# Exchange of softmax statistics between two key layouts in a conformer and dilated-attention block

## The chip, the cores and the metric

The kernel runs on one core of a Trainium2 chip. Its time is the device time of one execution in microseconds (us); the runs of a kernel are given by their median.

## The reference

The program computes one block on 1024 tokens with 1024 features, in 32-bit floats: an RMS norm, one input projection, a convolution branch with a gate, an attention branch, a merge of the two through sigmoid gates, and a feed-forward part with a short convolution. The change lies in the attention branch. There, 16 heads of 64 features attend in three groups of (window, dilation), and the groups are mixed by a softmax of their log-sums:

```python
for window, dilation in DILATION_GROUPS:          # (128, 1), (512, 4), (2048, 16)
    o_g, lse_g = dilated_window_attention(q, k, v, slopes, window, dilation)
...
mix = jax.nn.softmax(jnp.stack(lses), axis=0)
o = jnp.einsum('gbsh,gbshd->bshd', mix, jnp.stack(outs))
```

This is one softmax over all keys that any group admits, with the number of groups that admit a key as its weight. The kernel computes it in this form: its mask holds the logarithm of that number and the distance penalty.

## The kernel before, in words

**Precision.** A 32-bit product is made of three products of rounded halves (high by high, high by low, low by high); `split` (line 83) makes a high part on ACT (L85) and the low part on DVE (L86).

**Attention** runs in a loop of slots (from line 1106): 16 heads, two halves of 512 queries, four slots each, so eight slots ("places" 0 to 7) a head, and a tail of 13 slots. In its slot a query tile of 128 is scored on PE (`score`, L924 and L925); DVE adds the mask and takes the least value (L928); ACT takes the exponential and its sum (`powers`, L966). Twelve slots later (`BACK`) the weights are transposed on PE (`flip`, L1014), split, and multiplied by the values one slot on (`weigh`, L1051 and L1052). Between these, projection products of another branch fill PE (`fill`).

The queries of the second half (512 to 1023) meet two kinds of keys, in two layouts. *Near* keys are scored with queries in natural order: tile i, partition p is query 128 i + p. *Far* keys, the first half, are met only at distances that are multiples of four; they are scored by residue, so that partition j, column r is query 4 j + r. POOL copies the residue form of query and keys (`by_residue`, L921). The far scores are place 4, the near ones places 5 to 7. So each query of the second half has two maxima and two sums, in two layouts, and each layout needs those of the other to scale its weights:

- `own[h]` holds the statistics of head h, `own[h][:, 0]` of near and `own[h][:, 1]` of far rows, four pairs to a partition; `other[h]` is to hold the same queries' statistics from the other layout. Both have two buffers.
- `give` (L985) writes one layout's statistics to a scratch tensor in DRAM, and `take` (L989) reads them back in the other layout: 4 KB each, 8 bytes an element on the side of the near layout, 32 on that of the far one. They are called in the slot that made them: far at place 4, near at place 7.
- `combine` (L994 to L999) forms the factors, on DVE with one exponential on ACT, at place 6 of the next head; `times` (L969) scales the weights on POOL, and the far weights are flipped two slots later.

**Output.** `result` copies a finished half of a head to SBUF and writes it out with two transfers of 64 partitions (L1064), one for each half of the values' precision, into two DRAM tensors. `o_fetch` reads two feature blocks of 128 from each of the two, 512 tokens wide (L90 for the one, L152 for the other), and `o_step` adds and splits them (L1089, L1085, L1082).

**What sets the order.** ACT, DVE and PE run in the order of the text (`manual_schedule`). SP, which issues nearly all transfers, and POOL are ordered by a planner that simulates the program and issues what its simulation holds ready; each engine then runs its list in order, so an instruction that waits holds up all behind it. The head loads (`head`, L152 and L749) are six of 256 KB and the mask, with two buffers each; the program asks for those of head h + 1 at place 1 of head h, and for the values (`values`) at place 5.

Of the kernel before, what the change touches and what calls it, by code (L numbers as in the profile page):

```python
# [13 lines left out]
F32 = mybir.dt.float32  # L14
F32R = mybir.dt.float32r
AF = mybir.ActivationFunctionType
ALU = mybir.AluOpType
# [4 lines left out]
P = 128  # L22
D = 1024
T = 1024
KT = D // P
H = 16
DH = 64
# [8 lines left out]
FRONT = (1, 1, 1, 1, 0, 1, 1, 1)  # L36
BEHIND = (1, 0, 0, 0, 1, 0, 1, 0)
BACK = 12
START = (1, 1, 1, 1, 0, 0, 0, 0, 0, 0, 0, 0)
TAIL = (1, 1)  # L40
PLAIN = (10, 11)
# [17 lines left out]
def block_kernel(ctx: ExitStack, tc: tile.TileContext, x, xT, x0, g2, pack, mask,  # L59
                 w_first, w_ch, w_qkv, w_co, w_ao, w_o, w_up, w_down, out):  # L60
    nc = tc.nc
    act, dve, pool, pe, sp = nc.scalar, nc.vector, nc.gpsimd, nc.tensor, nc.sync

    cst = ctx.enter_context(tc.tile_pool(name="cst", bufs=1))
    wp = ctx.enter_context(tc.tile_pool(name="wp", bufs=1))
    psA = ctx.enter_context(tc.tile_pool(name="psA", bufs=2, space=PSUM))
    psB = ctx.enter_context(tc.tile_pool(name="psB", bufs=4, space=PSUM))
    dr = ctx.enter_context(tc.tile_pool(name="dr", bufs=1, space=DRAM))
# [14 lines left out]
    def split(hi, lo, src):  # L83

        act.activation(hi, src, AF.Copy)  # L85
        dve.tensor_tensor(out=lo, in0=src, in1=hi.bitcast(F32), op=ALU.subtract)  # L86

    def stage(src, name):
        raw = wp.tile([P, 1024], F32, tag="raw", bufs=4, name=f"raw_{name}")
        sp.dma_start(raw.rearrange("p (a b) -> p a b", a=src.shape[1]) if len(src.shape) == 3 else raw, src)  # L90
        return raw
# [59 lines left out]
    def fetch(dst, src):  # L151
        sp.dma_start(dst.bitcast(F32), src.bitcast(F32))  # L152
# [2 lines left out]
    dq = [[dr.tile([P, 4, T], F32R, name=f"dq{i}_{a}") for a in range(2)] for i in range(2)]  # L155
    dk = [[dr.tile([P, 4, T], F32R, name=f"dk{i}_{a}") for a in range(2)] for i in range(2)]
    dv = [dr.tile([T, 8, P], F32R, name=f"dv{i}") for i in range(2)]
    dst_ = [[dr.tile([512, 2], F32, name=f"dst{i}_{h}") for h in range(H)] for i in range(2)]
    dh = dr.tile([P, KT, T], F32, name="dh")
    db12 = [dr.tile([P, 4, 512], F32R, name=f"db12_{i}") for i in range(2)]  # L160
    dgate = [dr.tile([P, T], F32, name=f"dgate{i}") for i in range(16)]
    da = dr.tile([P, KT, T], F32, name="da")
    dya = [dr.tile([P, T], F32, name=f"dya{i}") for i in range(8)]
    do_ = [dr.tile([P, KT, T], F32, name=f"do{i}") for i in range(2)]
    dff = [dr.tile([P, T], F32, name=f"dff{i}") for i in range(FT)]
    dx2 = [dr.tile([P, D], F32, name=f"dx2_{i}") for i in range(8)]
    dform = [[dr.tile([P, 1024], F32R, name=f"dform{f}_{i}") for i in range(7)] for f in range(3)]
# [136 lines left out]
    if True:  # L304
# [156 lines left out]
        a, b = range(4), range(4, 8)  # L461
# [174 lines left out]
        for ch in range(6):  # L636
            kind, g8 = ch % 3, ch // 3
            wpieces = [wpiece(w_qkv[kind * 2 + g8, :, 2 * j : 2 * j + 2, :], f"qkv{ch}_{j}") for j in range(4)]
            for tt in range(8):
# [3 lines left out]
                if len(tails) > LAG:  # L643
                    t = tails.pop(0)
# [251 lines left out]
    if True:  # L896
# [80 lines left out]
        own, other = {}, {}  # L977
# [2 lines left out]
            own[h] = ready2("own", [P, 2, 4, 2], F32, 2, f"own_{h}")  # L980
            other[h] = ready2("other", [P, 2, 4, 2], F32, 2, f"other_{h}")

        def give(h, layout):
            d = dst_[layout][h]
            sp.dma_start((near_of, far_of)[layout](d), own[h][:, layout])  # L985

        def take(h, layout):
            d = dst_[1 - layout][h]
            sp.dma_start(other[h][:, layout], (near_of, far_of)[layout](d))  # L989

        def combine(h):
            o, t = own.pop(h), other.pop(h)
# [14 lines left out]
        def flip(h, half, group):  # L1007
            pp = bank_ps(f"pp_{h}_{half}_{group[0]}")
            ph = ready2("ph", [P, 512], F32R, 3, f"ph_{h}_{half}_{group[0]}")
            pl = ready2("pl", [P, 512], F32R, 3, f"pl_{h}_{half}_{group[0]}")  # L1010
            uses = []

            def turn(n, pt):
                pe.transpose(pp[:, n * P : (n + 1) * P], pt, ident)  # L1014

            if group == ("far",):
                for r in range(4):
                    turn(r, pts[h, "far", r][0])
                    uses.append((("far", r), slice(r * P, (r + 1) * P)))
                c = slice(0, 512)  # L1020
            else:
                used = []
                for kt in group:
                    q0 = max(kt, 4 * half)
                    q1 = 5 if kt == 3 and half else 4 * half + 4
                    first = 0 if kt == 3 and half else 1 if kt % 4 == 3 else q0 - 4 * half
                    for n, i in enumerate(range(q0, q1)):
                        turn(first + n, pts[h, i][0][:, (kt - lowest(i)) * P : (kt - lowest(i) + 1) * P])
                    cols = slice(first * P, (first + q1 - q0) * P)
                    uses.append(((kt, slice((q0 - 4 * half) * P, (q1 - 4 * half) * P)), cols))  # L1030
                    used.append(cols)
                c = slice(min(u.start for u in used), max(u.stop for u in used))
            order, runs = ((lambda t: t, lambda t: t) if group == ("far",) else
                           (by_fourth, lambda t: t.rearrange("p (i r a) -> p i r a", r=4, a=32)))
            split(runs(ph[:, c]), runs(pl[:, c]), order(pp[:, c]))
            return h, half, group, ph, pl, uses

        outs, read_out = {}, {}
# [15 lines left out]
            return (h, half) if last else None  # L1054

        def result(h, half):
            r = (h % 2) * DH
            o = outs.pop((h, half))
            cs = slice(half * 512, half * 512 + 512)
            tmp = ready2("ot", [P, 512], F32, 2, f"ot_{h}_{half}")  # L1060
            read_out[h, half] = act.activation(tmp.rearrange("p (i a r) -> p i a r", i=4, r=4),
                                               o.rearrange("p (i r a) -> p i a r", i=4, r=4), AF.Copy)
            for i in range(2):
                sp.dma_start(do_[i][r : r + DH, h // 2, cs], tmp[i * DH : (i + 1) * DH, :])  # L1064

        def fill(n):
            for _ in range(n):
# [3 lines left out]

        def o_fetch(half, k):
            cs = slice(half * 512, half * 512 + 512)
            raw = stage(do_[0][:, k : k + 2, cs], f"o_{half}{k}").rearrange("p (a b) -> p a b", a=2)
            hi, lo = (oT[i][half][:, k : k + 2, :] for i in range(2))
            fetch(lo, do_[1][:, k : k + 2, cs])
            return raw, hi, lo

        def o_step(new):
# [21 lines left out]
        with tc.manual_schedule(engines={ENG.Activation, ENG.DVE, ENG.PE}):  # L1101
            pend = []
            fill(1)
            for at in range(len(slots) + BACK + 1):
                count[2] += 1
                cur = slots[at] if at < len(slots) else None
                front, behind = (FRONT[at % 8], BEHIND[at % 8] + (START[at] if at < BACK else 0)) if cur else TAIL
                new = []
                if cur is not None:
                    h, half, n = cur  # L1110
                    place = at % 8
                    if place == 4:
                        statistics(h)
                    if place == 5:
                        values(h)
                    if place == 1 and h + 1 < H:
                        tiles[h + 1] = head(h + 1)
                    new = score(h, tiles[h], SCORES[half][n])
                for unit in late:
                    share(*unit)  # L1120
                if len(pieces) > 2:
                    piece_high(2)
                fill(front)
                if cur is not None and place == 6 and h + 1 < H or at == 1:
                    by_residue(h + 1 if at > 1 else 0)
                flips = []
                if BACK <= at < len(slots) + BACK:
                    fh, fhalf, fn = slots[at - BACK]
                    if FLIPS[fhalf][fn]:
                        flips.append(flip(fh, fhalf, FLIPS[fhalf][fn]))  # L1130
                for w in pend:
                    done = weigh(*w) or done
                pend = flips
                late = []
                if done is not None:
                    result(*done)
                    done = None
                since = at - BACK + 2
                if 0 <= since < len(slots) and slots[since][1:] == (1, 0):
                    combine(slots[since][0])  # L1140
                for unit in new:
                    powers(*unit)
                if cur is not None and half == 0:
                    late = new
                elif cur is not None and n in (0, 3):
                    give(h, 1 if n == 0 else 0)
                    take(h, 0 if n == 0 else 1)
                if at == len(slots):
                    p2_cm.__exit__(None, None, None)
                    hb2.append(ctx.enter_context(tc.tile_pool(name="hb2a", bufs=1, reuse_waits="tile")))  # L1150
                    oT = [[hb2[0].tile([P, KT, 512], F32R, tag=f"hb{a}0", name=f"oT{a}0")] for a in range(2)]
                    heads = [o_fetch(0, k) for k in range(0, KT - 2, 2)]
                if at > len(slots):
                    o_step(heads)
                if at == len(slots) + BACK - 4:
                    heads.append(o_fetch(0, KT - 2))
                piece_low()
                fill(behind)
                piece_high(2)
            for _ in gates:  # L1160
                piece_low()
                piece_high()
                o_step(heads)
# [325 lines left out]
    if True:  # L1489
# [49 lines left out]
        for f in range(FT):  # L1539
# [12 lines left out]
            r = ready.pop(0)  # L1552
# [235 lines left out]
```

## Time and profile before

| | |
|---|---|
| runs, median (lowest to highest of 3) | 1788.17 us (1788.1 to 1790.8) |
| the profiled execution | 1791.29 us, span 1789.2 us, mean granted clock 0.983 |
| PE busy / DVE / ACT / POOL | 1744.3 / 1300.4 / 789.1 / 223.7 us |
| HBM read / written | 214.80 / 84.02 MB |

The span is the time from the first to the last instruction of the profiled execution. "Busy" counts an engine's instructions, without those that only wait or issue transfers. The granted clock is the share of TensorE's full rate that was let through. In a row of groups stand the source line, the engine, the operation and out<-in by the program's names; in a row of waits, who waited for whom, the total in us, the times and the longest. SPq is SP's queue of issues.

### The profile page before, as it was taken

The numbers are of one execution on the slowest core, as the hardware profiler recorded it, in microseconds if no ns is written. First come the engines' busy times: TensorE is split into PE (matmuls) and PEld (weight loads), VectorE is DVE, ScalarE is ACT, GpSimd is POOL, SyncE is SP. The second block draws the span as 40 slices with busy tenths as digits, with TensorE's granted clock in tenths as the row PEclk, the third lists the DMA queues.
The fourth block names the chain that finished last, engine by engine and source line by source line (L and its number), as shares of the span: only waits on it lengthen the run. The fifth ranks groups of instructions, "written<-read, shape, count | busy, mean of one in ns | idle before, by whom it ended". The sixth has DMA issues, their size and how long they took to land.

```text
span 1789.2 us, 22776 instructions
## 1 busy us (share of the span) xinstructions
PE 1744.3 (97%) x8003; PEld 1422.1 (79%) x8003; DVE 1300.4 (73%) x2098; ACT 789.1 (44%) x1351; POOL 223.7 (13%) x300
## 2 busy tenths in 40 slices
PE   9999999999999997889899999999999999999999
PEld 7888888888888786777677888888888888888887
DVE  5999999999866465655455764687777677689863
ACT  5421233223335565656554643454454454543431
POOL 0000231132000344334330000000000000000000
PEclk9999999999999998889899999999999999999999
DMA  9311145345537878877766867542222222389851
GB/s 375 133 45 48 52 130 167 104 139 168 194 117 240 272 181 203 216 180 176 187 161 227 291 225 277 185 149 83 83 83 83 83 81 85 119 319 343 285 181 47
DMA packets 189938, 300.33 MB, mean 168 GB/s; under 512 B 35072, under 2 KB 93056, under 8 KB 189312
## 3 DMA queue, kind: packets, MB, share of 16 engines
q1 hardware_dynamic: 187376, 292.46, 51.0%
q10 hardware_dynamic: 2448, 6.42, 0.9%
q8 instruction: 63, 1.03, 0.2%
q14 instruction: 51, 0.42, 0.1%
HBM read 214.80 MB, written 84.02 MB: 167 GB/s over the span
## 4 chain that ended last, share of the span: by engine, by line
PE 88%; DMA 8%; DVE 1%; POOL 1%; ACT 1%; issue 1%; SPq 0%; ACTq 0%; DVEq 0%; POOLq 0%
PE dx L1594 7%; PE xz L141 6%; PE xz L142 6%; PE xz L143 6%; PE dy L1594 5%; PE qkv L134 5%; PE qkv L136 5%; PE qkv L135 5%; DMA dst<-own 4%; PE y L142 2%; PE y L141 2%; PE y L143 2%; PE wo L135 2%; PE wo L134 2%; PE wo L136 2%; PE yb L117 2%
## 5 line engine op out<-in xcount | busy, mean ns | idle before, releaser
L134 PE MATMUL qkv<-hi_qkv,hT 128*128 128x512 f32 x384 | 153.1, 400 | 0.0
L135 PE MATMUL qkv<-lo_qkv,hT 128*128 128x512 f32 x384 | 151.8, 396 | 0.0
L136 PE MATMUL qkv<-hi_qkv,hT 128*128 128x512 f32 x384 | 151.7, 396 | 0.0
L1497 DVE SCALAR_TENSOR_TENSOR u<-u,pk 128x1023 f32<-128x1023 f32 x88 | 112.2, 1277 | 1.2 <-ACT u L1495 1.1
L86 DVE TENSOR_TENSOR pl<-pp,ph 128x512 fp32r<-128x512 f32 (+1 forms) x95 | 59.2, 623 | 70.3 <-ACT ph L85 69.8
L110 POOL TENSOR_TENSOR rs<-ss,mhalf 128x8 f32<-128x8 f32 x32 | 66.3, 2073 | 303.4 <-DVE ss L109 303.3
L584 DVE SCALAR_TENSOR_TENSOR cacc<-csum,both,cacc 128x512 f32<-128x512 f32 x120 | 89.4, 745 | 0.3
L584 DVE SCALAR_TENSOR_TENSOR cacc<-apad,pk,cacc 128x512 f32<-128x512 f32 x120 | 88.3, 745 | 0.0
L136 PEld LDWEIGHTS qkv<-hi_qkv,hT 128*128 128x128 f32 x384 | 72.0, 188 | 17.1
L135 PEld LDWEIGHTS qkv<-lo_qkv,hT 128*128 128x128 f32 x384 | 72.1, 188 | 16.4
L134 PEld LDWEIGHTS qkv<-hi_qkv,hT 128*128 128x128 f32 x384 | 72.0, 188 | 16.4
L86 DVE TENSOR_TENSOR lo_uv<-raw_uv,hi_uv 128x1024 fp32r<-128x1024 f32 x20 | 24.5, 1225 | 82.1 <-ACT hi_uv L85 82.1
L584 DVE SCALAR_TENSOR_TENSOR codd<-apad,pk,codd 128x513 f32<-128x513 f32 x112 | 83.7, 748 | 0.7 <-ACT codd L577 0.7
L85 ACT ACTIVATE ph<-pp 128x512 fp32r<-128x512 f32 (+1 forms) x95 | 51.5, 542 | 58.4 <-PE pp L1014 55.9
L142 PE MATMUL xz<-blk_t,hi_s3g 128*128 128x512 f32 x176 | 69.3, 394 | 0.0
L141 PE MATMUL xz<-blk_t,hi_s3g 128*128 128x512 f32 x176 | 69.3, 394 | 0.0
L143 PE MATMUL xz<-blk_t,lo_s3g 128*128 128x512 f32 x176 | 69.0, 392 | 0.0
L141 PE MATMUL xz<-h2left,hi_uv 128*128 128x512 f32 x176 | 68.9, 391 | 0.0
L143 PE MATMUL xz<-h2left,lo_uv 128*128 128x512 f32 x176 | 68.6, 390 | 0.0
L142 PE MATMUL xz<-h2left,hi_uv 128*128 128x512 f32 x176 | 68.5, 389 | 0.0
L1495 ACT ACTIVATE u<-u,pk 128x1024 f32<-128x1024 f32 x44 | 54.6, 1240 | 9.2 <-DVE u L1484 4.5
L117 PE MATMUL ya<-aT,hi_co 128*128 128x512 f32 x128 | 57.5, 449 | 0.0
(486 smaller groups left out, 5155.6 us busy)
## 6 DMA issues: line engine op xcount, KB each, us to landing
wr<-w_down SPq DMA_DIRECT2D x45, 512.0 KB, 6.0
gr<-dff SPq DMA_DIRECT2D x62, 256.0 KB, 5.3
raw_qkv<-w_qkv SPq DMA_DIRECT2D x24, 512.0 KB, 5.2
dff<-u SPq DMA_DIRECT2D x22, 512.0 KB, 2.6
raw_uv<-w_up SPq DMA_DIRECT2D x21, 512.0 KB, 3.2
raw_ug<-w_up SPq DMA_DIRECT2D x20, 512.0 KB, 3.2
dv<-v SPq DMA_DIRECT2D x16, 512.0 KB, 2.8
q<-dq SPq DMA_DIRECT2D x32, 256.0 KB, 5.5
```

The source lines that it names most:

```text
L86: dve.tensor_tensor(out=lo, in0=src, in1=hi.bitcast(F32), op=ALU.subtract)
L110: pool.tensor_tensor(out=dst, in0=tmp, in1=mhalf[:, : tmp.shape[1]], op=ALU.pow)
L117: pe.matmul(o, hi[:, k, :], ah[:, k, :], start=(k == 0), stop=False)
L134: pe.matmul(ps, ah, hi[:, k % 2, :], start=(k == 0), stop=False)
L135: pe.matmul(ps, ah, lo[:, k % 2, :], start=False, stop=False)
L136: pe.matmul(ps, al, hi[:, k % 2, :], start=False, stop=(k == KT - 1))
L141: pe.matmul(o, wh[:, k, :], bh[:, k, :], start=(start and k == 0), stop=False, skip_group_check=not start)
L142: pe.matmul(o, wh[:, k, :], bl[:, k, :], start=False, stop=False, skip_group_check=not start)
L143: end = pe.matmul(o, wl[:, k, :], bh[:, k, :], start=False, stop=(k == 3), skip_group_check=not start)
L584: dve.scalar_tensor_tensor(out=out_, in0=src[:, i : i + size], scalar=w(i), in1=out_, op0=ALU.mult, op1=ALU.add)
L1497: dve.scalar_tensor_tensor(out=acc[:, d:], in0=src[:, : T - d], scalar=w(2 - d), in1=acc[:, d:], op0=ALU.mult, op1=ALU.add)
L1594: pe.matmul(banks[n][:, cols], a[:, c], b[:, d], start=(start and i == 0 and m == 0), stop=(stop and i == nf - 1 and m == 2), skip_group_c ...
```

## The change

- The near statistics are no longer written to DRAM. `near_to_far` copies them from `own` to `other` within SBUF, in four transfers, one for each query tile, each to 32 partitions.
- The far statistics still go through DRAM (`far_out`, `far_to_near`). The write is placed one slot after the far scores (`ago` 1), the readback five slots after them (1 + `TAKE`). `near_to_far` stands one slot after the last near scores.
- The output tensor in DRAM is one, ordered by head and precision half; `result` writes 128 partitions in one transfer, and `o_fetch` reads with four transfers of 64 partitions instead of two of 128.
- The call of `split` in `flip` is written out.

```diff
+TAKE = 4
...
-    dst_ = [[dr.tile([512, 2], F32, name=f"dst{i}_{h}") for h in range(H)] for i in range(2)]
+    dst_ = [dr.tile([512, 2], F32, name=f"dst_{h}") for h in range(H)]
...
-    do_ = [dr.tile([P, KT, T], F32, name=f"do{i}") for i in range(2)]
+    do_ = dr.tile([H, 2, DH, T], F32, name="do")
...
-        def give(h, layout):
-            d = dst_[layout][h]
-            sp.dma_start((near_of, far_of)[layout](d), own[h][:, layout])
-
-        def take(h, layout):
-            d = dst_[1 - layout][h]
-            sp.dma_start(other[h][:, layout], (near_of, far_of)[layout](d))
+        def near_to_far(h):
+            for i in range(4):
+                sp.dma_start(other[h][32 * i : 32 * i + 32, 1], own[h][:, 0, i])
+
+        def far_out(h):
+            sp.dma_start(far_of(dst_[h]), own[h][:, 1])
+
+        def far_to_near(h):
+            sp.dma_start(other[h][:, 0], near_of(dst_[h]))
...
-            split(runs(ph[:, c]), runs(pl[:, c]), order(pp[:, c]))
+            act.activation(runs(ph[:, c]), order(pp[:, c]), AF.Copy)
+            dve.tensor_tensor(out=runs(pl[:, c]), in0=order(pp[:, c]), in1=runs(ph[:, c]).bitcast(F32), op=ALU.subtract)
...
-            for i in range(2):
-                sp.dma_start(do_[i][r : r + DH, h // 2, cs], tmp[i * DH : (i + 1) * DH, :])
+            sp.dma_start(do_[h].rearrange("i d t -> (i d) t")[:, cs], tmp)
...
-            raw = stage(do_[0][:, k : k + 2, cs], f"o_{half}{k}").rearrange("p (a b) -> p a b", a=2)
+            raw = wp.tile([P, 1024], F32, tag="raw", bufs=4, name=f"raw_o_{half}{k}").rearrange("p (a b) -> p a b", a=2)
...
-            fetch(lo, do_[1][:, k : k + 2, cs])
+            for i, t in ((0, raw), (1, lo)):
+                for e in range(2):
+                    fetch(t[e * DH : (e + 1) * DH],
+                          do_.rearrange("(a e) i d t -> e i d a t", e=2)[e, i, :, k : k + 2, cs])
...
-                elif cur is not None and n in (0, 3):
-                    give(h, 1 if n == 0 else 0)
-                    take(h, 0 if n == 0 else 1)
+                for ago, n0, send in ((1, 0, far_out), (1, 3, near_to_far), (1 + TAKE, 0, far_to_near)):
+                    if 0 <= at - ago < len(slots) and slots[at - ago][1:] == (1, n0):
+                        send(slots[at - ago][0])
```

More of the change, by code (lines that the diff above doesn't have):

```diff
@@ L1056, in result @@
         def result(h, half):
-            r = (h % 2) * DH
             o = outs.pop((h, half))
```

## The prediction

> **What bounds the kernel now.** I read the page first, for the stretch in which the kernel loses time, then the busy time by head, then the waits, then SP's timeline.
>
> ```profile
> span 1789.2 us, 22776 instructions
> PE 1744.3 (97%) x8003; PEld 1422.1 (79%) x8003; DVE 1300.4 (73%) x2098; ACT 789.1 (44%) x1351; POOL 223.7 (13%) x300
> PEclk9999999999999998889899999999999999999999
> PE 88%; DMA 8%; DVE 1%; POOL 1%; ACT 1%; issue 1%; SPq 0%; ACTq 0%; DVEq 0%; POOLq 0%
> ```
>
> PE is the bound nearly everywhere. The only slices (some 45 us each) with a granted clock below nine tenths are the 16th to 18th and the 20th: attention, which runs from about 600 to 960 us. There the chain of waits names DMAs. The table by stage, cut where the far scores of each head begin, shows what a head costs; here are seven stretches of one head, one of the worst, and all fourteen from 612.1 to 917.4 us.
>
> ```profile
> core 0: us, PE busy (x) PEld busy (x) DVE busy (x) ACT busy (x) POOL busy (x), PEclk, DMA share, GB/s
> 634.80:652.40 17.60, 17.56 (x108) 14.77 (x107) 11.60 (x42) 13.14 (x39) 8.57 (x15) 1.00 0.71 176
> 652.40:671.40 19.00, 17.83 (x107) 14.81 (x107) 12.03 (x42) 12.74 (x38) 9.82 (x16) 1.00 0.64 172
> 744.20:765.00 20.80, 19.55 (x107) 16.14 (x107) 12.71 (x44) 12.86 (x39) 9.85 (x16) 0.92 0.75 208
> 765.00:786.20 21.20, 19.12 (x107) 15.99 (x106) 11.93 (x42) 12.48 (x38) 9.18 (x15) 0.92 0.69 171
> 833.40:851.90 18.50, 18.01 (x107) 14.88 (x107) 12.18 (x42) 13.01 (x39) 9.87 (x16) 1.00 0.71 175
> 851.90:877.90 26.00, 21.11 (x106) 17.13 (x105) 12.78 (x42) 12.98 (x39) 9.16 (x16) 0.87 0.80 192
> 877.90:899.00 21.10, 19.66 (x108) 16.09 (x107) 11.16 (x42) 12.20 (x37) 8.96 (x15) 0.92 0.81 184
> 899.00:917.40 18.40, 18.16 (x107) 14.83 (x106) 9.95 (x40) 12.01 (x36) 8.89 (x15) 1.00 0.60 150
> 612.10:917.40 305.30, 270.65 (x1466) 222.24 (x1465) 169.55 (x591) 179.93 (x524) 127.80 (x211) 0.91 0.76 188
> ```
>
> Every head has the same 106 to 108 matmuls, yet it takes 17.6 to 26.0 us. Four heads ran at clock 1.00 and take 18.4 us on average, 17.9 of them PE busy: PE's floor for a head. The mean is 305.3 / 14 = 21.8. What lies above the floor is PE idle (305.30 - 270.65 = 34.7 us) and half clock (0.09 of 305.3 is some 27 us; the two overlap a little). The floor for all fourteen would be 14 x 17.9 = 251: there are 54 us to win here, and no more.
>
> The waits in attention (595 to 985 us) say what PE and SP wait for:
>
> ```profile
> SPq L989 <- DMA dst<-own: 137.6, 32, 6.3
> DVE both L994 <- DMA other<-dst: 27.7, 10, 4.7
> PE pp_far L1014 <- POOL pf L969: 17.0, 11, 2.9
> PE s L925 <- DMA kl<-dk: 8.3, 6, 3.6
> PE o L1052 <- DVE pl L86: 5.2, 4, 2.5
> PE s L924 <- DMA kh<-dk: 3.5, 2, 2.2
> ```
>
> PE waits for weights that POOL scales late (pp_far), because DVE's combination (L994) waits for statistics, and for late K loads. Both come through SP, and SP stands 137.6 us before the 32 readbacks of L989, until the write issued just ahead has landed. One head of SP's timeline:
>
> ```profile
> 662.04 0.68 SPq L985 DMA_DIRECT2D dst<-own  x1
> 668.08 0.38 SPq L989 DMA_DIRECT2D other<-dst  x1
> ...
> 673.23 0.58 SPq L985 DMA_DIRECT2D dst<-own  x1
> 673.85 0.56 SPq L152 DMA_DIRECT2D kh<-dk  x1
> 674.46 0.59 SPq L152 DMA_DIRECT2D kl<-dk  x1
> 678.76 0.34 SPq L989 DMA_DIRECT2D other<-dst  x1
> ```
>
> SP stands from 662.7 to 668.1 (far pair) and from 675.1 to 678.8 (near pair), 9.1 of the 23 us to the next far write. The near stop lies in the middle of the next head's K loads, and it makes the near statistics two legs long. So in attention **SP's order is the bound**, and PE's gaps follow from it.
>
> **What the clock does with the gaps.** Three stretches around one late pp_far:
>
> ```profile
> 682.50:684.60 2.10, 0.02 (x2) 0.02 (x1) 1.73 (x8) 1.72 (x5) 1.10 (x3) 1.00 0.98 253
> 684.60:685.60 1.00, 0.64 (x2) 0.26 (x2) 1.00 (x6) 1.00 (x5) 1.00 (x2) 1.00 1.04 280
> 685.60:689.00 3.40, 3.21 (x9) 2.65 (x10) 1.60 (x4) 1.94 (x6) 2.63 (x6) 0.51 0.73 230
> ```
>
> A gap of about 2.1 us is followed by 3.4 us at 0.51 of the clock, so a removed gap brings back more than its length. [...]
>
> **The change, part by part.** Rows for it (tiles, then landings; durations are min/median/max in ns, the last column of a landing row is the median in us):
>
> ```profile
> L985 SPq DMA_DIRECT2D dst<-own x32: 340/547/1957, 604.1 to 928.5; - x32
> L989 SPq DMA_DIRECT2D other<-dst x32: 325/352/377, 610.5 to 932.8; - x32
> L1064 SPq DMA_DIRECT2D do<-ot x62: 445/588/2696, 638.2 to 967.1; - x62
> L152 SPq DMA_DIRECT2D oT<-do x8: 360/504/808, 929.2 to 972.8; - x8
> L90 SPq DMA_DIRECT2D raw_o<-do x8: 366/505/686, 839.1 to 971.6; - x8
> L928 DVE DVE_READ_ACCUMULATOR2_ANT own<- x128: 81/83/85, 602.2 to 927.0; 128x1 f32 x128
> do<-ot SPq DMA_DIRECT2D x62, 128.0 KB, 6.2
> q<-dq SPq DMA_DIRECT2D x28, 256.0 KB, 5.5
> dst<-own SPq DMA_DIRECT2D x32, 4.0 KB, 5.9
> other<-dst SPq DMA_DIRECT2D x32, 4.0 KB, 2.0
> ```
>
> 1. Near statistics. One write, one stop and one readback become four transfers with nothing to read back. The stop goes: 137.6 / 32 = 4.3 us a head. SP issues four instead of two. No row has a transfer inside the chip; its issue lies between the fastest readback, 0.33, and the slowest write, 1.96 us; I take the write's median, 0.55 (same source tile). So 4 x 0.55 - 0.55 - 0.35 = +1.3 us a head (ends +0.4 and +6.9). It lands after 1.5 to 8.9 us, the ends of the two kinds of rows; I take 5.9, as for the 4 KB write, which lands no sooner than the 256 KB loads beside it. Its new wait is for ACT's exponentials of the slot before; behind it on SP are the next head's K and Q halves and the mask. The combination is six slots later, 6 x 18.4 / 8 = 13.8 us, so even 8.9 fits.
>
> 2. Far statistics. Write and readback stay, so the two issues are the same, and the question is where SP takes the readback. SP's order is the planner's, not the program's: the first raw_o fetch issues at 839.1 us, while the program places it behind the last scores (927.0). So four slots later in the text is no promise; I count the far stop as kept, 4.3 us a head. Kept, it is cheap: it falls before the next K loads have their buffers. Behind it stand the V loads, which have twelve slots, and the output.
>
> 3. Output. One issue instead of two, twice a head: 2 x 0.59 = -1.2 us a head. The bytes are the same.
>
> 4. Fetches of the output, four instead of two, eight times: 16 more issues of 0.50. The low parts in the tail of attention hold up DVE (the wait of L1052 for pl, 5.2 us in 4), so one issue more delays them: two such places, +1 us. The eight of the second half stand ahead of loads for a later product: +4 us on SP, hidden behind the first projection products, which fill PE; uncovered it would cost those 4 us.
>
> 5. The call of split in flip is written out as the same two instructions: nothing on ACT, DVE or PE. POOL's order may change; within a head it is 9 us busy of 18, and I take nothing.
>
> **Sum.** SP gets 4.3 + 1.2 - 1.3 = 4.2 us a head back, plus what the near statistics' second leg (the 2.0 us landing, and 0.35) no longer adds to combinations that wait: I take 4.6. No head falls below 18.4. The three at 20.8, 21.2 and 21.1 gain 2.4 + 2.8 + 2.7 = 7.9; the four at 73.5 together nothing; the seven others, 305.3 - 73.5 - 63.1 = 168.7 us or 24.1 each, go to 19.5, which is 32.2. That is 40 us, less 1 for the tail: **39**. Against the profiled execution (1791.3, of which span 1789.2) that is 1752; the median of the runs shown is 3.1 lower, so the forecast is 1788.2 - 39 = **1749 us**. What is late next is PE itself, in heavy heads still SP with its far stop.
>
> **Rivals.**
> - *All stops go* (far too, if the planner does put other transfers between): all heads reach the 17.9 floor, 54 us: 1734, and 1730 with a little from the head after 917. For: four heads already run within 0.6 of it. Against: the planner's free order, and the loads still land 5 us after buffers come free.
> - *The gaps shrink, the clock or POOL stays.* Either pp_far stays late, because POOL's residue copies wait for K loads ahead of it (17.0 of the 39 us that PE waits), or half clock has another cause and only idle comes back (34.7 of 62). Both leave about 0.56 of 40: 22 us, 1766. [...] Against: the gap and half-clock rows.
> - *Nothing gained*: the planner moves the K loads behind the four transfers and SP is as late as before: 1788.
> - *Slower: the four transfers back up SP.* Place: ahead of the second K halves. If each issue takes as long as the slowest write, 1.96 us, they hold SP 7.8 us where the near pair held it 0.55 + 4.3 + 0.35 = 5.2; less 1.2 for the output, that is 1.4 a head, in fourteen heads 20 us, and half as much again by clock: 1818. It decides from (5.2 + 1.2) / 4 = 1.6 us an issue. Against: the median is 0.55.
>
> **How the numbers follow.** Forecast (1738 to 1757) 0.52; all stops go 0.11; partial (1757 to 1780) 0.22; nothing 0.05; slower 0.10. A measurement of this kernel tells about 0.2% (3.6 us) from no change. Faster 0.85, same 0.05, slower 0.10. The range takes the forecast, the partial case to 1777 and half of the case above it, from 1728.
>
> **What would show it.** Right: SP's wait for dst<-own falls from 137.6 to about 69 us or less; the copies from own to other issue in some 0.55 us; combinations no longer wait 27.7 us; PEclk in slices 16 to 20 rises to nine; heads take 18 to 20 us. Wrong: issues of over 1.6 us; a new wait of SP for ACT's exponentials of several us a head; K loads behind the four transfers with PE still waiting for kl; or the half clock without gaps.

## The result and the profile after

The changed kernel takes 1761.26 us (median of 4, 1759.65 to 1762.69) against 1788.13 us for the kernel before in the same session: 0.9846 of it, with a 95% interval of 0.9829 to 0.9863. It is faster by 27 us; 39 were forecast (1749, range 1728 to 1777). In a later session the kernel before took 1799.18 us and the changed one 1763.18: 0.9804 (0.9786 to 0.9822). The kernel before differs by 11 us between the two sessions, the changed one by 2. Why is not settled: in all four later sessions, on three chips, the kernel before took 1798.0 to 1799.2 us. So below, kernels of different sessions are compared by their ratios to the kernel before beside them.

The page of the changed kernel: PE and the granted clock.

```profile
span 1758.8 us, 22866 instructions
PE 1726.9 (98%) x8003; PEld 1409.3 (80%) x8003; DVE 1305.8 (74%) x2098; ACT 788.9 (45%) x1351; POOL 225.2 (13%) x300
PEclk9999999999999999999999999999999999999999
PE 88%; DMA 5%; DVE 2%; ACT 2%; SPq 1%; POOL 1%; issue 1%; ACTq 0%; DVEq 0%; POOLq 0%
```

No slice is below nine tenths any more. The table by stage, cut at the far scores of each head as before (the columns are those of the prediction's table), for two of the shortest heads, the three longest, and all fourteen:

```profile
629.20:646.20 17.00, 17.00 (x107) 14.72 (x106) 11.15 (x42) 13.15 (x39) 8.49 (x15) 1.00 0.80 201
721.40:742.60 21.20, 19.39 (x106) 16.12 (x106) 14.33 (x43) 12.83 (x39) 9.73 (x16) 0.92 0.83 221
742.60:763.40 20.80, 19.26 (x107) 16.09 (x106) 13.21 (x42) 12.41 (x38) 9.20 (x16) 0.92 0.82 214
819.60:845.80 26.20, 21.15 (x108) 17.31 (x107) 12.73 (x42) 13.11 (x39) 9.55 (x16) 0.87 0.86 209
864.00:881.00 17.00, 17.00 (x107) 14.84 (x106) 9.95 (x40) 12.08 (x36) 8.88 (x15) 1.00 0.57 146
611.80:881.00 269.20, 253.57 (x1466) 210.91 (x1465) 175.06 (x591) 180.11 (x524) 129.35 (x211) 0.97 0.83 212
```

The fourteen heads take 269.2 us where they took 305.3: 36.1 less. PE idle there fell from 34.7 to 15.6 us (269.20 - 253.57), and the mean clock rose from 0.91 to 0.97. But from the start of the sixteenth head to the end of the span the changed kernel takes 1758.8 - 881.0 = 877.8 us, and the kernel before 1789.2 - 917.4 = 871.8. So 36 us were won in the heads and **6 given back after them**, which makes the 30.4 us between the two spans (0.3 lies ahead of the heads). The waits of 595 to 985 us show both sides:

```profile
SPq L992 <- DMA dst<-own: 63.8, 15, 6.4
DVE both L997 <- DMA other<-dst: 0.9, 1, 0.9
PE pp_far L1017 <- POOL pf L970: 9.1, 10, 1.5
PE yb L118 <- DVE gg L1209: 7.3, 1, 7.3
PE s L926 <- DMA kl<-dk: 0.5, 1, 0.5
```

SP stands half as long before a readback (63.8 for 137.6 us). Combinations hardly wait (0.9 for 27.7), late K loads are gone (0.5 for 8.3), late far weights halved (9.1 for 17.0). New is one wait of 7.3 us for yb, a projection product after attention.

### The profile page after: what moved, and what is told of

The parts are those of the page before. It is cut to its first block, busy times and chain, and to the rows that moved or that the text cites. A ratio compares the mean times of both kernels' runs of the same rounds, so it can differ in the third digit from the quotient of the medians.

```text
span 1758.8 us, 22866 instructions
## 1 busy us (share of the span) xinstructions
PE 1726.9 (98%) x8003; PEld 1409.3 (80%) x8003; DVE 1305.8 (74%) x2098; ACT 788.9 (45%) x1351; POOL 225.2 (13%) x300
## 4 chain that ended last, share of the span: by engine, by line
PE 88%; DMA 5%; DVE 2%; ACT 2%; SPq 1%; POOL 1%; issue 1%; ACTq 0%; DVEq 0%; POOLq 0%
PE dx L1599 7%; PE xz L142 6%; PE xz L143 6%; PE xz L144 6%; PE dy L1599 5%; PE qkv L135 5%; PE qkv L136 5%; PE qkv L137 5%; PE y L143 2%; PE y L142 2%; PE y L144 2%; PE wo L136 2%; PE wo L135 2%; PE wo L137 2%; DMA oT<-do 1%; DMA kl<-dk 1%
## 5 line engine op out<-in xcount | busy, mean ns | idle before, releaser
L118 PE MATMUL yb<-oT,hi_ao 128*128 128x512 f32 x128 | 50.9, 398 | 7.3 <-DVE gg L1209 7.3
```

## The experiments

Each experiment is one kernel. "Heads" is the time from the first far score of the second head to that of the sixteenth, "rest" from there to the end of the span, both of the profiled execution, of which there is one for each kernel. Ratios are to the kernel before in the same session. Of the kernel before there is a trace from the first session only.

| kernel | median us | ratio (95%) | heads | rest |
|---|---|---|---|---|
| before (first session) | 1788.1 | | 305.3 | 871.8 |
| changed (first session) | 1761.3 | 0.9846 (0.9829 to 0.9863) | 269.2 | 877.8 |
| changed again | 1763.2 | 0.9804 (0.9786 to 0.9822) | 270.3 | 878.3 |
| near alone | 1760.2 | 0.9786 (0.9770 to 0.9801) | 276.9 | 870.7 |
| output alone | 1795.2 | 0.9979 (0.9968 to 0.9990) | 296.7 | 880.8 |
| TAKE 0 | 1767.1 | 0.9822 (0.9808 to 0.9837) | 277.5 | 878.7 |
| tensor by precision first | 1883.3 | 1.0471 (1.0455 to 1.0487) | 375.9 | 892.0 |
| stop kept | 1814.6 | 1.0090 (1.0071 to 1.0109) | 318.5 | 881.7 |
| far on chip too | 1750.6 | 0.9727 (0.9702 to 0.9752) | 261.8 | 877.8 |
| changed, old output | 1756.6 | 0.9767 (0.9748 to 0.9785) | 272.7 | 870.1 |
| fetches on two queues | 1767.2 | 0.9826 (0.9807 to 0.9846) | 275.2 | 878.4 |
| old output, far on chip | 1747.7 | 0.9726 (0.9704 to 0.9748) | 260.7 | 869.8 |
| the same, dya on SP | 1744.9 | 0.9704 (0.9685 to 0.9723) | 262.4 | 870.1 |
| old output, narrow fetches | 1770.4 | 0.9838 (0.9812 to 0.9864) | 277.5 | 880.7 |

**Which half pays: near alone, output alone.** To the kernel before was added only one part of the change: the near copies here, the one output tensor with its fetches there.

```diff
-                elif cur is not None and n in (0, 3):
-                    give(h, 1 if n == 0 else 0)
-                    take(h, 0 if n == 0 else 1)
+                elif cur is not None and n == 0:
+                    give(h, 1)
+                    take(h, 0)
+                elif cur is not None and n == 3:
+                    near_to_far(h)
```

> The kernel before with the near statistics alone sent on chip; far pair, output and fetches as before. Theory (SP's stop behind the near write is what pays, and the output half gives back in the tail what it wins in the heads): 1755 to 1767 us, SP's wait for dst<-own falls from 137.6 to some 65 us, PE's 7.3 us wait of yb does not appear. Rival (the single output transfer is what pays): above 1780 us.

> The kernel before with the output tensor, the single output transfer and the four fetches alone; both statistics pairs as before. Theory: 1780 to 1794 us, some 1 us a head won and 6 to 8 us lost behind the sixteen fetches of the second half, where PE waits for yb. Rival (the single output transfer is what pays): below 1772 us.

Near alone took 1760.2 us. Its ratio, 0.9786, cannot be told from that of the whole change in the later session (0.9804; the intervals overlap); SP's wait is 66.0 us, and there is no wait of yb. Output alone won 0.2%: its heads are short of 305.3 by 8.6 us, and its rest is 9.0 us longer, with PE's wait for yb at 6.6 us. Its median is 1 us above the expected range, in a session in which the kernel before was 11 us slower. So the near half is what pays. Whether it pays by the stop or by statistics that come sooner, these two kernels do not tell; the stop kept, below, does.

**The measure for the second group.** The changed kernel again.

> The changed kernel as it is, as the measure for the others of this group. Both theories: 0.980 to 0.987 of the kernel before.

It came out at 0.9804, within that.

**Stop or late statistics: the stop kept.** Behind the four transfers SP also writes the near statistics to a scratch tensor and reads them into a tile that nothing uses. What the output needs travels the short way, but SP stands.

```diff
+        def stop(h):
+            sp.dma_start(near_of(dummy[h]), own[h][:, 0])
+            sp.dma_start(p2b.tile([P, 4, 2], F32, tag="idle", bufs=2, name=f"idle_{h}"), far_of(dummy[h]))
...
-                for ago, n0, send in ((1, 0, far_out), (1, 3, near_to_far), (1 + TAKE, 0, far_to_near)):
+                for ago, n0, send in ((1, 0, far_out), (1, 3, near_to_far), (1, 3, stop), (1 + TAKE, 0, far_to_near)):
```

> The changed kernel, with a write of the near statistics to DRAM and a readback into a tile that nothing reads added behind the four transfers, so that SP stands again while the statistics still go the short way. Theory (the time comes from SP standing): 15 to 30 us above the changed kernel, SP's wait for dst and dummy some 60 us more. Rival (it comes from statistics that arrive sooner): within 5 us of the changed kernel.

It took 1814.6 us, 51 above the changed kernel beside it: the theory's direction, but far more than its 15 to 30. SP's waits, PE's for K loads, and the fourteen heads in this kernel:

```profile
SPq L997 <- DMA dst<-own: 73.1, 15, 6.0
SPq L991 <- DMA dummy<-own: 56.4, 16, 5.0
PE s L926 <- DMA kh<-dk: 13.8, 8, 2.6
PE s L927 <- DMA kl<-dk: 8.7, 10, 1.6
611.70:930.20 318.50, 278.52 (x1466) 228.16 (x1464) 164.42 (x591) 180.04 (x524) 126.00 (x211) 0.88 0.75 179
```

The heads grew by 48 us (318.5 for 270.3), while SP stands 60 us more (129.5 for 69.2). Late statistics are not the cause: DVE's combinations wait for them once, 4.6 us, and for a far pair. What is late is K: PE waits 22.5 us for it, where the changed kernel waited 0.5 for kl. SP stands nearly as long as in the kernel before (129.5 for 137.6), and issues eight transfers of statistics a head where that one issued four, so this kernel is slower still. That was the size the expectation missed: it priced the stop as the change had won it, and left out the issues. How much of the 51 us the two added issues take, and how much the standing, no kernel separates.

**Does the place in the text matter: TAKE 0.**

```diff
-TAKE = 4
+TAKE = 0
```

> The changed kernel with the far readback asked for in the slot of its write (TAKE 0 instead of 4). Theory (the planner sets SP's order, the text position does not): 1757 to 1766 us, as the changed kernel, with the same 60 to 68 us of SP wait for dst<-own. Rival (the four slots pay): above 1770 us and more wait of SP.

It took 1767.1 us, 1 us above the expected range; its ratio cannot be told from that of the changed kernel (the intervals overlap). SP's wait is nearly the same (72.5 us in 16, beside 69.2 in 15), if above the expected 60 to 68. What differs is the first head of the fourteen: 23.1 us at a granted clock of 0.85, where the changed kernel has 17.4 (at 1.00) and 18.5. There the planner's order did change: of SP's 911 issues one stands elsewhere in its list, the readback of the head before. So the four slots matter in one head out of fourteen; everywhere else the planner's order stood.

**Is the far stop free: far on chip too.** The far statistics go in four transfers, the other way round.

```diff
-        def far_out(h):
-            sp.dma_start(far_of(dst_[h]), own[h][:, 1])
...
-            sp.dma_start(other[h][:, 0], near_of(dst_[h]))
+            for i in range(4):
+                sp.dma_start(other[h][:, 0, i], own[h][32 * i : 32 * i + 32, 1])
...
-                for ago, n0, send in ((1, 0, far_out), (1, 3, near_to_far), (1 + TAKE, 0, far_to_near)):
+                for ago, n0, send in ((1, 0, far_to_near), (1, 3, near_to_far)):
```

> The changed kernel with the far statistics sent on chip as well, in four transfers, and no DRAM for either. Theory (each stop of SP costs): 4 to 12 us below the changed kernel, SP's wait for dst gone. Rival (the far stop stands where nothing is urgent): within 3 us of the changed kernel, or above it by the two further issues a head, 2 x 0.6 us.

It took 12.6 us less than the changed kernel (1750.6 for 1763.2), just beyond the expected 4 to 12; SP's wait for dst is gone, and the fourteen heads take 261.8 us. SP's timeline of the changed kernel shows what the far stop holds up:

```profile
651.02 0.63 SPq L989 DMA_DIRECT2D dst<-own  x1
651.86 0.61 SPq L986 DMA_DIRECT2D other<-own  x1
656.95 0.37 SPq L992 DMA_DIRECT2D other<-dst  x1
657.42 0.49 SPq L153 DMA_DIRECT2D kh<-dk  x1
```

and PE's in the same head, when K's buffer was last read:

```profile
653.63 0.28 PE L926 MATMUL s<-kl,q 128*128 128x256 f32 x1
```

The buffers were free at 653.9 us, and the K load went out at 657.4, behind the readback for which SP had stood since 652.5. So the far stop does lie across the K loads.

**Where the tail's 6 us go: four kernels.** The first was to undo the narrow fetches: a tensor ordered by precision half, then head, so that a fetch is two transfers of 128 partitions and the output stays one.

```diff
-    do_ = dr.tile([H, 2, DH, T], F32, name="do")
+    do_ = dr.tile([2, H, DH, T], F32, name="do")
...
-            sp.dma_start(do_[h].rearrange("i d t -> (i d) t")[:, cs], tmp)
+            sp.dma_start(do_[:, h, :, cs], tmp)
...
-                for e in range(2):
-                    fetch(t[e * DH : (e + 1) * DH],
-                          do_.rearrange("(a e) i d t -> e i d a t", e=2)[e, i, :, k : k + 2, cs])
+                fetch(t, do_[i].rearrange("(a e) d t -> (e d) a t", e=2)[:, k : k + 2, cs])
```

> The changed kernel with the output tensor ordered by precision half, then head, so that a fetch is two transfers of 128 partitions again and the output stays one transfer. Theory (the sixteen narrow fetches of the second half hold DVE and through it PE): 1750 to 1757 us, PE's wait for yb under 2 us. Rival (the wait comes from the bytes, or from SP being early): 1759 to 1764 us with the wait still there.

It took 4.7% more than the kernel before, and both theories were wrong about its time. What the DMA engines moved, in 40 slices of 630 to 900 us, and one stretch of those in which the rate is low:

```profile
GB/s 203 118 37 180 202 174 38 135 232 187 42 168 215 249 99 110 185 232 169 120 137 228 252 52 119 202 228 52 92 200 235 56 86 202 186 83 81 174 251 84
697.90:703.20 5.30, 5.30 (x30) 4.69 (x29) 2.44 (x8) 3.02 (x8) 2.54 (x5) 0.83 0.13 50
```

The rate breaks down to 37 to 56 GB/s again and again, with PE waiting for K loads (34.1 us in 5). The new write has 2 as its outermost size, where it was 128. In the stretch shown the share of busy DMA engines is 0.13 (the last number but one), by my estimate two of the sixteen engines at a time (0.13 x 16 = 2.1). But no row here names the engine of a packet, and whether the size of 2 sets this share is not shown. PE's wait for yb is gone in this kernel, as the theory said; with everything else late, that settles nothing, and the fetches' question stayed open.

The second put back the old output and fetches; the third issued half of the second half's fetches from ACT's queue.

```diff
-    do_ = dr.tile([H, 2, DH, T], F32, name="do")
+    do_ = [dr.tile([P, KT, T], F32, name=f"do{i}") for i in range(2)]
...
-            sp.dma_start(do_[h].rearrange("i d t -> (i d) t")[:, cs], tmp)
+            r = (h % 2) * DH
+            for i in range(2):
+                sp.dma_start(do_[i][r : r + DH, h // 2, cs], tmp[i * DH : (i + 1) * DH, :])
...
-                for e in range(2):
-                    fetch(t[e * DH : (e + 1) * DH],
-                          do_.rearrange("(a e) i d t -> e i d a t", e=2)[e, i, :, k : k + 2, cs])
+                fetch(t, do_[i][:, k : k + 2, cs])
```

```diff
-                    fetch(t[e * DH : (e + 1) * DH],
-                          do_.rearrange("(a e) i d t -> e i d a t", e=2)[e, i, :, k : k + 2, cs])
+                    (act if half and i else sp).dma_start(
+                        t[e * DH : (e + 1) * DH].bitcast(F32),
+                        do_.rearrange("(a e) i d t -> e i d a t", e=2)[e, i, :, k : k + 2, cs].bitcast(F32))
```

> The changed kernel with the output tensors, the two output transfers and the two fetches of before. Theory (the output half gives back in the tail what it wins in the heads): within 5 us of the changed kernel, with PE's 7 us wait of yb gone and the fourteen heads 5 to 9 us longer. Rival (the single output transfer is worth more than its tail): 6 us or more above it.

> The changed kernel with the eight fetches of low parts of the second half issued from ACT's queue instead of SP's. Theory (the tail is lost because SP issues sixteen narrow fetches one after the other): 3 to 8 us below the changed kernel's 1761 to 1763, and PE's wait for yb under 4 us. Rival (the bytes or their landing set the tail): within 2 us of it, the wait still 6 to 8 us.

The old output is 6.6 us **faster** than the changed kernel, 1.6 more than expected: its heads are 2.4 us longer (5 to 9 expected), its rest 8.2 us shorter, and the wait of yb is gone. The two queues changed nothing in the rest (878.4 us, wait of yb 7.7): the theory that SP's issuing sets the tail fell. (The median, 1767.2, lies 4 us above the changed kernel's, outside the rival's 2 us as well; the ratios cannot be told apart.) The DMA engines were full either way. The first 14.6 us of the second half's fetches, in the kernel before, the changed one, that with the old output and that with two queues:

```profile
967.80:982.40 14.60, 14.60 (x67) 12.07 (x66) 8.08 (x8) 4.07 (x5) 0.00 (x0) 1.00 1.01 362
```

```profile
926.90:941.50 14.60, 14.60 (x66) 12.09 (x65) 5.30 (x5) 2.72 (x3) 0.00 (x0) 1.00 1.00 254
```

```profile
933.00:947.60 14.60, 14.60 (x66) 12.07 (x65) 8.05 (x7) 3.70 (x5) 0.00 (x0) 1.00 1.01 357
```

```profile
934.20:948.80 14.60, 14.60 (x66) 12.11 (x65) 4.26 (x4) 2.62 (x3) 0.00 (x0) 1.00 1.02 245
```

The last two numbers are the DMA share and GB/s: busy all the time in each, but 245 to 254 GB/s with fetches of 64 partitions and 357 to 362 with 128. Width or the tensor's order in DRAM? The fourth kernel has the old tensors and output, and cuts only the fetches in two (shown against the kernel with the old output).

```diff
-            fetch(t, do_[i][:, k : k + 2, cs])
+            for e in range(2):
+                r = slice(e * DH, (e + 1) * DH)
+                fetch(t[r], do_[i][r, k : k + 2, cs])
```

> The changed kernel with the output tensors and the two output transfers of before, but each fetch still cut into 64 partitions (four transfers a step, as in the changed kernel). Theory (the width of the fetches sets their rate in the tail, where the DMA engines are busy all the time): PE's wait for yb is 6 to 8 us again, the stretch of the second half's fetches moves some 250 GB/s, 0.979 to 0.984 of the kernel before. Rival (the order of the output tensor in DRAM sets it): no wait of yb, some 360 GB/s, 0.975 to 0.978.

```profile
938.90:953.50 14.60, 14.60 (x66) 12.09 (x65) 5.95 (x5) 2.57 (x3) 0.00 (x0) 1.00 1.00 246
```

246 GB/s, a rest of 880.7 us, and the wait of yb back at 7.5: cutting the fetches does it, whatever the order of the tensor. A cut fetch is also half as large, 256 KB for 512, but that is not the cause. The loads of the gates and of dya that follow the fetches in the changed kernel are 256 KB too, with 128 partitions, and with them the DMA engines move 380 GB/s:

```profile
960.00:966.00 6.00, 6.00 (x27) 4.97 (x26) 3.40 (x6) 2.92 (x4) 0.00 (x0) 0.96 1.04 380
```

So it is the width: fetches of 64 partitions move 0.7 of the rate of those of 128 (254 for 362 GB/s), and why is not shown.

**Put together.** The old output with far on chip (shown against the kernel with the old output; `far_to_near` is that of far on chip), and then with the stores of dya that ACT issues moved to SP.

```diff
-                for ago, n0, send in ((1, 0, far_out), (1, 3, near_to_far), (1 + TAKE, 0, far_to_near)):
+                for ago, n0, send in ((1, 0, far_to_near), (1, 3, near_to_far)):
```

```diff
-                (sp if c < 4 else act).dma_start(dya[c][:, half * 512 : half * 512 + 512], ya)
+                sp.dma_start(dya[c][:, half * 512 : half * 512 + 512], ya)
```

> The changed kernel with the output of before and both statistics on chip. Theory (the two gains of 12.6 and 6.6 us add up): 1741 to 1748 us. Rival (without the single output transfer SP is the bound again, so that they don't add up): 1750 us or more.

> The same as the one before it, and the eight stores of dya that ACT issues go to SP's queue. Theory (ACT stands some 3 to 5 us once, before its first store, and PE with it, followed by half clock): 2 to 8 us below the one before it. Rival (the wait moves to SP): within 2 us.

The first took 1747.7 us, inside the theory's range. But its ratio, 0.9726, is that of far on chip with the single output (0.9727), so the medians do not show that the two gains add up. Of the gain of the old output the profiled executions show the 8 us in the rest (869.8 for 877.8); they are the fastest of four runs here and the slowest of four there. The second took 1744.9, which is 2.7 us less; the two intervals overlap, and its profiled heads are no shorter (262.4 for 260.7), so its gain is not shown either, though the 2.6 us that ACT stood before its first store are gone. At 0.9704 of the kernel before it is the fastest kernel here, 18 us below the changed one in its later session. Its span is 1744.3 us, with PE busy for 1723.3.

## Why the prediction was right, and where not

- *SP's order is the bound in attention.* Right, and shown twice: with the stop kept, the statistics on chip bring nothing, and PE waits 22.5 us for K loads; with the stops gone, the heads come to 261 us.
- *Near statistics.* The stop went as forecast, 137.6 to 63.8 us. The four issues cost more, the landing less than I took:

```profile
L986 SPq DMA_DIRECT2D other<-own x64: 548/603/1713, 605.0 to 892.0; - x64
other<-own SPq DMA_DIRECT2D x64, 1.0 KB, 3.7
dst<-own SPq DMA_DIRECT2D x16, 4.0 KB, 6.0
```

  0.60 us an issue for 0.55, 3.7 us to land for 5.9. The planner does not issue them as a block: the first goes out beside the far write (651.86 us above), as soon as its tile is scored. The slower rival needed 1.6 us an issue.
- *Far statistics.* That the planner and not the text sets the place was right, but for one head. "Kept, it is cheap: it falls before the next K loads have their buffers" was wrong: it costs 12.6 us. I had read the order of SP's list, not when the buffers fell free.
- *Output, -1.2 us a head.* Oversized. With the output of before, the fourteen heads are 2.4 us longer in all, but that kernel has the wide fetches too. With narrow fetches on both sides the single output is worth 7.2 us (277.5 for 270.3), 0.5 a head. Each is one profiled execution.
- *Heads, -40.* 36.1 measured, but not where the sum had put it. The seven slow heads won 29.5 us for 32.2 forecast, the three at 21 us 2.9 for 7.9, and the four fast ones 3.7 for nothing, so that the total came this close partly by luck. "No head falls below 18.4" was wrong: five do, and two take 17.0 at full clock. So the floor of 17.9 a head, or 251, was too high as well.
- *Fetches.* This is the step that failed: "hidden behind the first projection products, which fill PE; uncovered it would cost those 4 us". I counted issues and took a transfer's rate as given. During the sixteen narrow fetches the DMA engines move 254 GB/s instead of 362; the last sum of the output starts 23.6 us after the last output store (950.1 - 926.5), for 15.3 before (982.4 - 967.1). In DVE's timeline the first product's evacuation (955.11) stands behind it:

```profile
950.12 1.22 DVE L1094 TENSOR_TENSOR raw_o<-raw_o,oT 128x1024 f32<-128x1024 f32 x1 [3.98 <-DMA oT<-do]
951.26 2.43 DVE L1087 TENSOR_TENSOR oT<-raw_o,oT 128x1024 fp32r<-128x1024 f32 x2
954.50 0.69 DVE L1202 TENSOR_TENSOR gg<-gg 128x512 f32<-128x512 f32 x1 [0.81 <-ACT gg L1200]
955.11 0.69 DVE L1209 TENSOR_TENSOR gg<-yb,gg 128x512 f32<-128x512 f32 x1
```

  and PE, its four buffers full, waits 7.3 us. Forecast +1, measured +6.0 behind the heads. That is not all. The fourth kernel of the tail and the one with the old output differ in the fetches alone, 0.9838 and 0.9767 of the kernel before: some 13 us, of which the traces show 10.6 in the rest and 4.8 in the heads. In the heads the loss lies in the one that takes 26.2 us in the changed kernel. There it is 27.5 for 21.5, and ACT, with PE behind it, stands 7.5 for 3.3 us before its first store of dya. What ties that wait to the fetches is not shown.
- *The sum.* 36.1 - 6.0 against 40 - 1: the time fell into the range although the fetches were mis-sized. The profiled execution of the kernel before lay 3.1 us above its median, so the medians show 27.
- *Rivals.* The half clock went with the gaps in most heads, as the trace of before had it: eleven of the fourteen ran at a granted clock of 1.00, where four did; "all stops go" is what the far-on-chip kernels did, short of the floor.

## What to carry to other kernels

A write to DRAM with its readback right behind it, on the queue that also issues the loads, cost more here than its bytes: for 4 KB, SP stood 4.3 us before each readback of the kernel before (137.6 us in 32), and loads behind a readback were late (the K load at 657.4 us, with its buffers free at 653.9). Look at what falls free during the stop before calling it hidden. When a transfer is re-cut to save issues, look at the shape on the other end too: here one issue saved per store was paid for by fetches of half the width, 254 GB/s for 362, where the DMA engines were full (share 1.00 and 1.01).

## What was not expected of the hardware

Fetches of 64 partitions moved 245 to 254 GB/s where those of 128 moved 357 to 362, at a DMA share of 1.00 to 1.02 in both, and a second queue did not help. In the kernel with a store whose outermost size is 2, the rate of all transfers broke down to 37 to 56 GB/s in slices of 6.75 us, at a DMA share of 0.13 in the stretch shown. Copies within SBUF, of 1 KB each, landed in 3.7 us (median), beside loads of the heads of 256 to 512 KB that took 4.5 to 7.6.
